# Hybrid convolution and sparse-attention block: intermediates stored in DRAM as high and low parts by their producers

## Chip, core and metric

One core of a Trainium2 chip runs the kernel as a single program. The metric is device time in microseconds (us), as the median of three executions. One further execution was recorded by the hardware profiler; all rows below come from it. Engine names are those of the profile: PE (TensorE), DVE (VectorE), ACT (ScalarE), POOL (GpSimd) and SP (the engine that issues almost all DMA transfers).

## What is computed

The input is x, 1024 tokens by 1024 channels, in float32. Cut to what matters here:

```python
h = rmsnorm(x, norm_in_g)
q, k, v..., gates, z_nsa, glu_in, z_conv, merge_g = split(h @ w_in)
o_nsa  = nsa_attention(q, k, v, gates, rel_bias)     # compressed + selected + window
y_nsa  = (o_nsa * silu(z_nsa)) @ w_nsa_proj
c      = silu(layernorm(dwconv31(a * sigmoid(b))))   # a, b = split(glu_in)
y_conv = (c * silu(z_conv)) @ w_conv_proj
g_conv, g_nsa = split(sigmoid(merge_g))
out    = rmsnorm(x + (g_conv * y_conv + g_nsa * y_nsa) @ w_out, norm_f_g)
```

There are 16 heads of width 64 in 2 key/value groups. All of it is held to float32 accuracy.

## The kernel before

**Three matmuls for one.** TensorE takes its operands here as `F32R` tiles, and one float32 product is built from three of them: weights high times activations high, high times low and low times high. The high part of a tile is an ACT `Copy` into an F32R tile; the low part is the float32 tile minus the high one, made by `sub_low` (line 68; the profile shows it as L69). Activations lie transposed, channels on partitions and tokens along the free axis, and are worked in two halves of 512 tokens (`hf`). A matrix of activations is four tiles, (high, low) by (half 0, half 1), each 128 x 8 x 512, taken from the tags b00, b01, b10 and b11 (`big_pair`).

**Stages.** Up to about 540 us of the span the kernel normalises x, projects it through `w_in` and runs the convolution. From there to about 1310 us the attention runs in eight steps (g, qp). TensorE's gaps between attention matmuls are filled with other projections, issued at a low priority: first the last columns of `w_in` (`late_columns`, L697), then `w_conv_proj` (`projections`, L964), then `w_nsa_proj` (`nsa_early`, L976). The bank for these fillers, `fb`, is one PSUM tile with one buffer. After 1310 us come the last part of `w_nsa_proj` and `w_out`.

**Order of the work.** Every engine runs its instructions in the order written by a scheduler at build time, from priorities in the code (`LOW`, `AHEAD`) and from `issue_after`, which ties the fillers of `nsa_early` to attention steps. SP issues its DMAs in one such order, too: a DMA that waits holds back all behind it.

**Intermediates in DRAM.** Four of them are written by one stage and read back by a later one as matmul operands:

- `YD`, the convolution path times its gate: made per half column in `late_columns` (L708 tanh on ACT, L710 on DVE, L712 the product with `ct` on POOL, L713 the store), read by `projections`.
- `OD`, the gated attention output: made per pair of heads in `attend` (L949 to L955, `ot`, one buffer), stored at L961, read for `nsa_early`.
- `ND`, the merged sum of both branches: made in `merged` (L677; L684 on DVE, L685 on POOL), stored at L982; half 0 is read back for `w_out` as `mh0` and `ml0`, half 1 as a partial sum (`mt`).
- `MD` and `GD` hold a partial sum and the gates, and are read as plain float32.

The tiles `mg`, `ct`, `gt`, `mt` and `sq` share the tag "ev", a ring of three buffers (L74): a new tile waits until the third one before it is done with. Reading YD, OD or ND half 0 goes through `load_half`: a DMA of a quarter (512 KB), an ACT copy to the high tile, and a subtraction on POOL (on DVE for `ml0`) that turns the loaded tile into the low part:

```python
nc.sync.dma_start(f(l), src[q * 256:(q + 1) * 256].rearrange("(k p) n -> p k n", p=P))
with tc.high_priority(offset=ahead):
    nc.scalar.activation(h, f(l), AF.Copy)
    sub_low(eng, l, f(l), h)
```

In `select` (L751 to L774 here) DVE scores the blocks of keys of the next attention step: row sums, a reciprocal, products over tiles of 128 x 312 and more, and the eight largest. DVE also makes the low parts `tl` of the transposed attention weights (L69), which TensorE needs for the attention output (L908).

Of the kernel before, what the change touches and what calls it, by code (L numbers as in the profile page):

```python
# [8 lines left out]
F32 = mybir.dt.float32  # L9
F32R = mybir.dt.float32r  # L10
AF = mybir.ActivationFunctionType
ALU = mybir.AluOpType
# [4 lines left out]
P = 128  # L17
S = 1024
D = 1024
KT = D // P  # L20
NB = S // P
HALF = 512
# [30 lines left out]
LOW = -1000000  # L53
AHEAD = 1000
# [4 lines left out]
def hybrid_block(ctx, tc, x, norm_in_g, w_in, pos_ck, w_ck1, w_ck2, pos_cv, w_cv1, w_cv2,  # L59
                 rel_bias, conv_w, conv_b, conv_ln_g, conv_ln_b, w_conv_proj, w_nsa_proj,  # L60
                 w_out, norm_f_g, cst, buckets, out):
    nc = tc.nc
    x, w_in, out = x[0], w_in[0], out[0]

    def f(ap):
        return ap.bitcast(F32)

    def sub_low(eng, low, full, high):
        eng.tensor_tensor(low, full, f(high), op=ALU.subtract)  # L69
# [4 lines left out]
    ev = ctx.enter_context(tc.tile_pool(name="ev", bufs=3, reuse_waits="tile"))  # L74
# [16 lines left out]
    OD = dram.tile([D, S], F32, name="OD")  # L91
    MD = dram.tile([D, S], F32, name="MD")
    CD = dram.tile([D, S], F32, name="CD")
    ND = dram.tile([2, D, HALF], F32, name="ND")
    TD = dram.tile([NH, P, 384], F32, name="TD")
    TV = dram.tile([NH, 384], F32, name="TV")

# [123 lines left out]
    with ExitStack() as c1:  # L221
# [302 lines left out]
        with ExitStack() as c2:  # L524
# [9 lines left out]
            for t in range(NB):  # L534
                ps = bank()
# [125 lines left out]
    def fbank():  # L661
        return pf.tile([P, HALF], F32, tag="f", name="fb")

    def load_half(pair, src, quarters, eng, ahead):
        ah, al = pair
        for q in quarters:
            ks = slice(2 * q, 2 * q + 2)
            h, l = ah[:, ks, :], al[:, ks, :]
            nc.sync.dma_start(f(l), src[q * 256:(q + 1) * 256].rearrange("(k p) n -> p k n", p=P))
            with tc.high_priority(offset=ahead):  # L670
                nc.scalar.activation(h, f(l), AF.Copy)
                sub_low(eng, l, f(l), h)

    def columns(w):
        return [w[0][:, t * P:(t + 1) * P] for t in range(KT)]

    def merged(t, hf, ps, prev, raise_, eng):  # L677
        sl = slice(hf * HALF, (hf + 1) * HALF)
        gt = ev.tile([P, HALF], F32, tag="ev", name="gt")
        nc.sync.dma_start(gt, GD[D + t * P:D + (t + 1) * P, sl])  # L680
        mt = ev.tile([P, HALF], F32, tag="ev", name="mt")
        nc.sync.dma_start(mt, prev)
        with tc.high_priority(offset=raise_):
            nc.vector.scalar_tensor_tensor(gt, gt, 1.0, ps, op0=ALU.add, op1=ALU.mult)  # L684
        eng.tensor_tensor(gt, gt, mt, op=ALU.add)  # L685
        return gt

    nsa_cols = columns(w_nsa_proj)
    oa = []
# [1 line left out]
    with att as c3:  # L691
# [5 lines left out]
        def late_columns():  # L697
            todo = [(C_ZC, t) for t in range(KT)] + [(C_MG, j) for j in range(EARLY, 2 * KT)]
            cols = [w_in[:, c + j * P:c + (j + 1) * P] for c, j in todo]
            for n, hf, ps in ends_halved(cols, hT, fbank, (False, True)):  # L700
                kind, j = todo[n]
                rows_j, sl = slice(j * P, (j + 1) * P), slice(hf * HALF, (hf + 1) * HALF)
                mg = ev.tile([P, HALF], F32, tag="ev", name="mg")
                if kind == C_ZC:
                    ct = ev.tile([P, HALF], F32, tag="ev", name="ct")
                    nc.sync.dma_start(ct, CD[rows_j, sl])
                with tc.high_priority(offset=-LOW):
                    nc.scalar.activation(mg, ps, AF.Tanh, scale=0.5)  # L708
                    if kind == C_ZC:
                        nc.vector.scalar_tensor_tensor(mg, mg, 1.0, ps, op0=ALU.add, op1=ALU.mult)  # L710
                if kind == C_ZC:
                    nc.gpsimd.tensor_tensor(mg, mg, ct, op=ALU.mult)  # L712
                    nc.sync.dma_start(YD[rows_j, sl], mg)  # L713
                else:
                    nc.sync.dma_start(GD[rows_j, sl], mg)

        with tc.high_priority(offset=LOW):
            late_columns()
# [195 lines left out]
        def attend(g, qp, sel, ahead):  # L914
            q, masks, pcs = sel
            nxt = None
            for hp in range(HG // 2):
# [26 lines left out]
                for u, (br, c, b) in enumerate(ones_):  # L944
# [4 lines left out]
                ot = ap.tile([P, 256], F32, tag="ot", name="ot", bufs=1)  # L949
# [6 lines left out]
                if (g, qp) == steps[-1]:  # L956
                    kk, to = g * 4 + hp, slice(qp % 2 * 256, (qp % 2 + 1) * 256)
                    nc.scalar.activation(oa[0][1][:, kk, to], ot, AF.Copy)
                    sub_low(nc.vector, oa[1][1][:, kk, to], ot, oa[0][1][:, kk, to])
                else:  # L960
                    nc.sync.dma_start(OD[fr, tk], ot)  # L961
            return nxt

        def projections():  # L964
            ya = big_pair()
            for hf in range(2):
                load_half((ya[0][hf], ya[1][hf]), YD[:, hf * HALF:(hf + 1) * HALF], range(4), nc.gpsimd, AHEAD)
            for t, hf, ps in ends_halved(columns(w_conv_proj), ya, fbank, (True, True)):
                sl = slice(hf * HALF, (hf + 1) * HALF)
                gt = ev.tile([P, HALF], F32, tag="ev", name="gt")  # L970
                nc.sync.dma_start(gt, GD[t * P:(t + 1) * P, sl])
                with tc.high_priority(offset=-2 * LOW):
                    nc.vector.scalar_tensor_tensor(gt, gt, 1.0, ps, op0=ALU.add, op1=ALU.mult)
                nc.sync.dma_start(MD[t * P:(t + 1) * P, sl], gt)

        def nsa_early():  # L976
            for hf in range(2):
                for t, src in enumerate(nsa_cols):
                    rows_t = slice(t * P, (t + 1) * P)
                    gt = merged(t, hf, mm_half(src, oa, hf, fbank(), (0, 1) if hf == 0 else (0,)),  # L980
                                MD[rows_t, hf * HALF:(hf + 1) * HALF], -2 * LOW, nc.gpsimd)
# [15 lines left out]
        for n, (g, qp) in enumerate(steps):  # L997
            if n in (2, 4, 6):
                load_bt(g)
            if n == 4:  # L1000
                base[0] = 0
                load_kv(0, 1, 1)
            if n == 6:
                load_kv(1, 0, 0)
                load_kv(1, 1, 1)
            if n == 6:
                with tc.high_priority(offset=2 * LOW):
                    projections()
                    oa.extend(big_pair())
                    load_half((oa[0][0], oa[1][0]), OD[:, 0:HALF], range(4), nc.gpsimd, AHEAD)  # L1010
                    load_half((oa[0][1], oa[1][1]), OD[:, HALF:S], range(2), nc.gpsimd, AHEAD)
                    while turns[0] < 0:
                        turns.pop(0)
                        next(early)
            if n == 7:
                with tc.high_priority(offset=2 * LOW):
                    load_half([m[:, :, 0:256] for m in (oa[0][1], oa[1][1])], OD[:, HALF:HALF + 256], range(2, 4),
                              nc.gpsimd, AHEAD)
# [9 lines left out]
    def ebank():  # L1028
        return pe.tile([P, HALF], F32, tag="e", name="eb")
# [1 line left out]
    gf = ep.tile([P, D], F32, name="gf", bufs=1)  # L1031
    mh = [big.tile([P, KT, HALF], F32R, tag="b00", name="mh0"), ep.tile([P, KT, HALF], F32R, name="mh1", bufs=1)]
    ml = [big.tile([P, KT, HALF], F32R, tag="b10", name="ml0"), ep.tile([P, KT, HALF], F32R, name="ml1", bufs=1)]
    load_half((mh[0], ml[0]), ND[0], range(4), nc.vector, 0)
    wo = [[ep.tile([P, KT, HALF], F32R, name=f"wo{part}{dh}", bufs=1) for part in range(2)] for dh in range(2)]

    def load_out(dh, q):
# [4 lines left out]
        sub_low(nc.vector, wo[dh][1][:, ks, :], raw, wo[dh][0][:, ks, :])  # L1042

    for t, src in enumerate(nsa_cols):
        gt = merged(t, 1, mm_half(src, oa, 1, ebank(), (1,)), ND[1, t * P:(t + 1) * P, :], 0, nc.vector)
        nc.scalar.activation(mh[1][:, t, :], gt, AF.Copy)
        sub_low(nc.vector, ml[1][:, t, :], gt, mh[1][:, t, :])
# [82 lines left out]
```

## Time and profile before

| | us |
|---|---|
| median of 3 executions | 1430.57 |
| lowest, highest | 1430.08, 1430.83 |
| the profiled execution's own time | 1430.01 |
| span from its first to its last instruction | 1428.2 |
| mean granted TensorE clock | 0.994 of full speed |

A row of the profile gives start and length in microseconds and names the engine, the line of the code, and output and inputs of the instruction. "Waits" are the stretches in which an engine stood still, with the instruction that ended the wait. In windows each engine has its busy time, with the number of instructions in brackets; PEclk is the granted TensorE clock, and the last two columns are the mean busy share of the DMA engines and what they moved in GB/s.

### The profile page before, as it was taken

To read this page: it belongs to the slowest core of one execution; us is meant where nothing else is said; L and a number is where in the kernel's file an instruction comes from. 1 tells how busy PE (TensorE), PEld (TensorE's weight loads), DVE (VectorE), ACT (ScalarE), POOL (GpSimd) and SP (SyncE) were. 2 spreads that over 40 slices of the span, in tenths; PEclk is the share of its full clock that TensorE was granted. 3 is DMA by queue.
4 is the path that set the end of the run, shared out by engine and by line. 5 is a ranking of instruction groups with operands and counts; after the bars stand their busy time and mean duration, and the time that the engine had idled before them with its cause. 6 is when DMAs were issued, how large, how long until landed. Compare 5 with 4: busy or idle time off the path is not lost.

```text
span 1428.2 us, 22832 instructions
## 1 busy us (share of the span) xinstructions
PE 1391.0 (97%) x7516; PEld 1197.0 (84%) x7516; DVE 1032.8 (72%) x2367; ACT 675.4 (47%) x1441; POOL 709.6 (50%) x809
## 2 busy tenths in 40 slices
PE   6999999999999999999999999989999999999997
PEld 5788888888988787889888889879989898898786
DVE  5699999999965714767676685586678557886732
ACT  6321112113144424766656666755555766675421
POOL 2323224234155825765555455785545887884111
PEclk9999999999999999999999999999999999999999
DMA  5333424346283743343333322453253543534632
GB/s 174 72 104 106 128 69 133 113 132 176 81 199 111 236 122 113 119 128 101 96 94 89 115 83 59 130 170 115 89 148 119 178 129 123 182 115 153 219 119 89
DMA packets 189167, 179.55 MB, mean 126 GB/s; under 512 B 12549, under 2 KB 146773, under 8 KB 189048
## 3 DMA queue, kind: packets, MB, share of 16 engines
q1 hardware_dynamic: 186984, 174.94, 40.7%
q10 hardware_dynamic: 2064, 3.15, 0.7%
q8 instruction: 60, 0.98, 0.3%
q14 instruction: 59, 0.48, 0.1%
HBM read 128.20 MB, written 52.98 MB: 127 GB/s over the span
## 4 chain that ended last, share of the span: by engine, by line
PE 82%; DVE 6%; DMA 4%; issue 3%; POOL 3%; ACT 2%; SPq 0%; ACTq 0%; DVEq 0%; POOLq 0%
PE mm L122 9%; PE mm L124 9%; PE mm L123 9%; PE sb L835 7%; PE tb L882 7%; PE fb L122 4%; PE fb L123 4%; PE fb L124 4%; PE ob L908 3%; PE ob L907 3%; PE fb L134 3%; PE fb L135 3%; PE fb L136 3%; PE eb L1063 2%; PE eb L1062 2%
## 5 line engine op out<-in xcount | busy, mean ns | idle before, releaser
L69 POOL TENSOR_TENSOR wl<-raw,wh 128x512 fp32r<-128x512 f32 x184 | 244.9, 1332 | 371.4 <-ACT wh L111 360.1
L353 DVE SCALAR_TENSOR_TENSOR ca<-u,vec,ca 128x1024 f32<-128x1024 f32 x232 | 284.0, 1281 | 0.8
L122 PE MATMUL mm<-act,wh 128*128 128x512 f32 x640 | 252.9, 395 | 1.5 <-DVE zs L566 1.3
L123 PE MATMUL mm<-act,wh 128*128 128x512 f32 x640 | 249.6, 390 | 0.0
L124 PE MATMUL mm<-act,wl 128*128 128x512 f32 x640 | 247.2, 390 | 0.0
L870 ACT ACTIVATE p<-p,ac 128x640 f32<-128x640 f32 (+7 forms) x256 | 187.5, 735 | 88.0 <-DVE ac L862 82.4
L111 ACT ACTIVATE wh<-raw 128x512 fp32r<-128x512 f32 x184 | 115.4, 628 | 232.0 <-PE mm L123 157.9
L875 POOL TENSOR_SCALAR p<-p,rcx,gates 128x640 f32<-128x640 f32 (+7 forms) x256 | 201.4, 797 | 8.9
L69 DVE TENSOR_TENSOR tl<-tb,th 128x512 fp32r<-128x512 f32 (+1 forms) x272 | 158.0, 591 | 46.1 <-ACT th L886 44.5
L835 PE MATMUL sb<-k,q 128*128 128x384 f32 (+2 forms) x704 | 176.5, 350 | 2.5 <-DVE ac L862 1.5
L886 ACT ACTIVATE th<-tb 128x512 fp32r<-128x512 f32 (+1 forms) x272 | 135.0, 517 | 70.8 <-PE tb L882 66.6
L882 PE MATMUL tb<-ident,p 128*128 128x128 f32 x1056 | 165.1, 273 | 0.1
L122 PEld LDWEIGHTS mm<-act,wh 128*128 128x128 f32 x640 | 120.1, 188 | 27.6 <-DVE zs L566 1.8
L124 PEld LDWEIGHTS mm<-act,wl 128*128 128x128 f32 x640 | 120.1, 188 | 25.9 <-POOL wl L69 0.6
L123 PEld LDWEIGHTS mm<-act,wh 128*128 128x128 f32 x640 | 120.2, 188 | 24.7
L122 PE MATMUL fb<-act,wh 128*128 128x512 f32 x320 | 127.9, 400 | 2.5 <-ACT mg L708 1.3
L882 PEld LDWEIGHTS tb<-ident,p 128*128 128x128 f32 x1056 | 124.7, 140 | 4.7 <-DVE stl L69 0.3
L908 PE MATMUL ob<-tl,v 128*128 128x256 f32 x448 | 124.0, 297 | 4.1 <-DVE tl L69 3.8
L124 PE MATMUL fb<-act,wl 128*128 128x512 f32 x320 | 126.2, 394 | 0.0
L123 PE MATMUL fb<-act,wh 128*128 128x512 f32 x320 | 126.1, 394 | 0.0
L907 PE MATMUL ob<-th,v 128*128 128x256 f32 x448 | 124.2, 291 | 1.0 <-ACT th L886 0.9
L835 PEld LDWEIGHTS sb<-k,q 128*128 128x128 f32 x704 | 114.1, 189 | 12.8 <-DVE ac L862 2.8
(245 smaller groups left out, 2638.9 us busy)
## 6 DMA issues: line engine op xcount, KB each, us to landing
raw<-in_w_in_dram SPq DMA_DIRECT2D x128, 256.0 KB, 3.1
gt<-GD SPq DMA_DIRECT2D x40, 256.0 KB, 3.1
GD<-mg SPq DMA_DIRECT2D x32, 256.0 KB, 3.3
q<-QD SPq DMA_DIRECT2D x64, 128.0 KB, 3.6
raw<-in_w_nsa_proj_dram SPq DMA_DIRECT2D x32, 256.0 KB, 3.0
raw<-in_w_conv_proj_dram SPq DMA_DIRECT2D x24, 256.0 KB, 3.7
k<-KD SPq DMA_DIRECT2D x40, 128.0 KB, 3.5
xt<-in_x_dram SPq DMA_DIRECT2D x8, 512.0 KB, 6.2
```

Of the source, the lines that this page charges most:

```text
L69: eng.tensor_tensor(low, full, f(high), op=ALU.subtract)
L122: nc.tensor.matmul(ps, wh[:, k, :], mh[:, kk, :], start=(kk == 0), stop=False)
L123: nc.tensor.matmul(ps, wh[:, k, :], ml[:, kk, :], start=False, stop=False)
L124: nc.tensor.matmul(ps, wl[:, k, :], mh[:, kk, :], start=False, stop=(kk == KT - 1))
L353: nc.vector.scalar_tensor_tensor(dst, u, w, accs[e], op0=ALU.mult, op1=ALU.add)
L835: nc.tensor.matmul(s[:, 0:w], lhs, K[j][:, br, k0:k0 + w], start=(j == 0), stop=(j == 1))
L870: nc.scalar.activation(pt[:, 0:n], pt[:, 0:n], AF.Exp, bias=mn, scale=-1.0, accum_out=sm[:, b:b + 1])
L875: nc.gpsimd.tensor_scalar(pt[:, 0:n], pt[:, 0:n], rc[:, b:b + 1], gates[:, 2 * qp + b, gcol:gcol + 1], op0=ALU.mult, op1=ALU.mult)
L882: nc.tensor.transpose(tp[:, j * P:(j + 1) * P], src, ident)
L886: nc.scalar.activation(th, src, AF.Copy)
L907: nc.tensor.matmul(dst, lhs, th[:, sl], start=False, stop=False)
L908: last = nc.tensor.matmul(dst, lhs, tl[:, sl], start=False, stop=False)
```

## The change

YD and OD become arrays of two parts, high and low. ND keeps only half 1, and half 0 moves to a new array `NS` of two parts. The stage that makes a value also splits it (`split_store`) and stores both parts; the reader loads two tiles (`load_pair`) and does no arithmetic. The tiles on the ring "ev", `ot`, and a new tile `oh` (one buffer) become F32R. Where a high part needs a tile, a used one serves: `ct` for YD and `mt` for NS.

```diff
-    YD = dram.tile([D, S], F32, name="YD")
+    YD = dram.tile([2, D, S], F32, name="YD")
...
-    def load_half(pair, src, quarters, eng, ahead):
...
+    def load_pair(pair, src, quarters):
         for q in quarters:
+            for part in range(2):
+                nc.sync.dma_start(f(pair[part][:, 2 * q:2 * q + 2, :]),
+                                  src[part, q * 256:(q + 1) * 256].rearrange("(k p) n -> p k n", p=P))
+
+    def split_store(high, low, dst):
+        nc.scalar.activation(high, f(low), AF.Copy)
+        sub_low(nc.gpsimd, low, f(low), high)
+        nc.sync.dma_start(dst[0], f(high))
+        nc.sync.dma_start(dst[1], f(low))
...
-                    nc.gpsimd.tensor_tensor(mg, mg, ct, op=ALU.mult)
-                    nc.sync.dma_start(YD[rows_j, sl], mg)
+                    nc.gpsimd.tensor_tensor(f(mg), f(mg), f(ct), op=ALU.mult)
+                    split_store(ct, mg, YD[:, rows_j, sl])
...
-                    nc.sync.dma_start(OD[fr, tk], ot)
+                    oh = ap.tile([P, 256], F32R, tag="oh", name="oh", bufs=1)
+                    split_store(oh, ot_, OD[:, fr, tk])
...
-                    nc.sync.dma_start(ND[hf, rows_t, :], gt)
+                    if hf == 0:
+                        split_store(mt, gt, NS[:, rows_t])
+                    else:
+                        nc.sync.dma_start(ND[rows_t], f(gt))
...
-    load_half((mh[0], ml[0]), ND[0], range(4), nc.vector, 0)
+    load_pair((mh[0], ml[0]), NS, range(4))
```

**How instructions move.** Three places are shown, before and then after; the lines of the changed kernel are shifted by 3 or 4. First POOL, at the step in which the loads of YD used to be split; `wl<-raw,wh` makes a weight's low part, `p<-p,rcx,gates` scales attention weights, `act<-act` is the subtraction of `load_half`:

```order
L69 TENSOR_TENSOR wl<-raw,wh 128x512
L69 TENSOR_TENSOR act<-act 128x1024
L875 TENSOR_SCALAR p<-p,rcx,gates 128x640
L875 TENSOR_SCALAR p<-p,rcx,gates 128x768
L69 TENSOR_TENSOR act<-act 128x1024
L69 TENSOR_TENSOR wl<-raw,wh 128x512
L69 TENSOR_TENSOR act<-act 128x1024 x2
L771 TENSOR_TENSOR lt<-lt,gates 128x8x39
```

```order
L959 TENSOR_TENSOR ot<-ot,zt 128x256
L69 TENSOR_TENSOR wl<-raw,wh 128x512
L851 TENSOR_TENSOR cm<-bt,msk 128x256
L69 TENSOR_TENSOR ot<-ot,oh 128x256
L69 TENSOR_TENSOR wl<-raw,wh 128x512
L851 TENSOR_TENSOR cm<-bt,msk 128x256
L875 TENSOR_SCALAR rcx<-rcx 128x2
L878 TENSOR_SCALAR p<-p,rcx,gates 128x640
```

The subtractions on 128 x 1024 are gone, and a subtraction on 128 x 256 stands behind each product of `ot`. Second DVE at the same step, where `select` scores the blocks (L766, L767 and L770 before are L769, L770 and L773 after):

```order
L766 TENSOR_TENSOR lt<-lt,rc 128x8x39
L862 ISA p,ac<-sb,bt,ac 128x256
L862 ISA ac 128x1
L767 SCALAR_TENSOR_TENSOR lt<-lt 128x8x39
L751 TENSOR_REDUCE sm<-lt 128x8
L770 TENSOR_REDUCE ih<-lt 128x39
L69 TENSOR_TENSOR tl<-tb,th 128x512
L752 TENSOR_SCALAR sm<-sm 128x8
```

```order
L769 TENSOR_TENSOR lt<-lt,rc 128x8x39
L769 TENSOR_TENSOR lt<-lt,rc 128x8x47
L865 ISA p,ac<-sb,cm,ac 128x256
L865 ISA ac 128x1
L770 SCALAR_TENSOR_TENSOR lt<-lt 128x8x39
L770 SCALAR_TENSOR_TENSOR lt<-lt 128x8x47
L773 TENSOR_REDUCE ih<-lt 128x39
L773 TENSOR_REDUCE ih<-lt 128x47
```

The scoring of two blocks of queries, which was spread over some 30 rows, now stands together. Third SP, at the loads of `mh0` and `ml0`:

```order
L669 DMA ml_15074<-ND 128x2x512 x3
L103 DMA raw<-in_w_nsa_proj_dram 128x4x128
L982 DMA ND<-gt 128x512
L682 DMA mt<-MD 128x512
L680 DMA gt<-GD 128x512
L669 DMA ml_15074<-ND 128x2x512
```

```order
L668 DMA ml_15243<-NS 128x2x512
L668 DMA mh_15241<-NS 128x2x512 x2
L668 DMA ml_15243<-NS 128x2x512
L668 DMA mh_15241<-NS 128x2x512
L104 DMA raw<-in_w_nsa_proj_dram 128x4x128
L668 DMA ml_15243<-NS 128x2x512
L674 DMA NS<-mt 128x512
L675 DMA NS<-gt 128x512
L104 DMA raw<-in_w_nsa_proj_dram 128x4x128
L685 DMA mt<-MD 128x512
L668 DMA mh_15241<-NS 128x2x512
L683 DMA gt<-GD 128x512
L668 DMA ml_15243<-NS 128x2x512
```

Three loads ahead of the last store of half 0 have become six, and that store has become two.

In all, ACT loses 16 copies of quarters of YD and OD and 4 of ND and gains 24 copies on 128 x 512 and 28 on 128 x 256; POOL loses 16 subtractions of quarters and gains 24 on 128 x 512 and 28 on 128 x 256; DVE loses 4; SP issues 72 more DMAs (16 + 28 + 8 stores and 8 + 8 + 4 loads). TensorE's instructions are the same in number.

## Rows read from the trace of the kernel before

**Rows 1.** The page's first part: busy time of each engine over the span.

```profile
PE 1391.0 (97%) x7516; PEld 1197.0 (84%) x7516; DVE 1032.8 (72%) x2367; ACT 675.4 (47%) x1441; POOL 709.6 (50%) x809
```

**Rows 2.** What TensorE waited for, 545 to 1310 us: us, times, longest.

```profile
PE ob L908 <- DVE tl L69: 3.8, 4, 2.9
PE sb L835 <- DVE ac L862: 1.5, 3, 0.8
...
PE fb L122 <- ACT mg L708: 1.3, 2, 0.9
...
PE fb L122 <- DVE mg L710: 0.9, 2, 0.6
```

**Rows 3.** Windows: length, PE, PEld, DVE, ACT, POOL busy, PEclk, DMA share, GB/s.

```profile
940.00:945.40 5.40, 1.68 (x10) 1.00 (x8) 5.37 (x9) 3.66 (x7) 5.40 (x4) 0.86 0.54 185
945.40:950.90 5.50, 5.28 (x17) 4.24 (x18) 5.50 (x14) 1.52 (x3) 5.50 (x4) 0.52 0.29 91
...
1120.00:1140.00 20.00, 19.32 (x116) 16.64 (x116) 11.70 (x38) 13.67 (x30) 19.00 (x19) 1.00 0.53 170
```

**Rows 4.** Timeline of DVE, 939 to 953 us: start, length, engine, line.

```profile
939.47 0.39 DVE L752 TENSOR_SCALAR sm<-sm 128x8 f32<-128x8 f32 x1
...
941.46 2.24 DVE L767 SCALAR_TENSOR_TENSOR lt<-lt 128x312 f32<-128x312 f32 x1
...
945.26 1.91 DVE L752 TENSOR_SCALAR sm<-sm 128x8 f32<-128x8 f32 x1
...
952.27 0.54 DVE L767 SCALAR_TENSOR_TENSOR lt<-lt 128x376 f32<-128x376 f32 x1
```

**Rows 5.** Timeline of POOL, 936 to 950 us.

```profile
940.77 2.58 POOL L69 TENSOR_TENSOR act<-act 128x1024 fp32r<-128x1024 f32 x1
...
944.79 4.68 POOL L69 TENSOR_TENSOR act<-act 128x1024 fp32r<-128x1024 f32 x2
```

**Rows 6.** Groups by line, 545 to 1310 us: busy us, mean ns, idle before and releaser.

```profile
L69 POOL TENSOR_TENSOR act<-act 128x1024 fp32r<-128x1024 f32 (+1 forms) x16 | 36.1, 2269 | 4.5 <-ACT act L671 4.4
L671 ACT ACTIVATE act<-act 128x1024 fp32r<-128x1024 f32 (+1 forms) x16 | 16.1, 1004 | 9.7 <-DMA act<-YD 4.9 <-DMA act<-OD 4.8
L69 DVE TENSOR_TENSOR ml<-ml,mh 128x1024 fp32r<-128x1024 f32 x4 | 5.3, 1336 | 0.9 <-ACT mh L671 0.9
L69 POOL TENSOR_TENSOR wl<-raw,wh 128x512 fp32r<-128x512 f32 x88 | 115.2, 1309 | 61.6 <-ACT wh L111 56.4 <-DMA ct<-CD 3.4
L955 POOL TENSOR_TENSOR ot<-ot,zt 128x256 f32<-128x256 f32 x31 | 22.9, 740 | 31.1 <-DVE ot L954 30.7
```

**Rows 7.** The page's costliest groups: the ACT copy on 128 x 512.

```profile
L111 ACT ACTIVATE wh<-raw 128x512 fp32r<-128x512 f32 x184 | 115.4, 628 | 232.0 <-PE mm L123 157.9
```

**Rows 8.** The chain that ended last, near 1120 us: start, us, what.

```profile
1119.83 2.39 POOL act L69
```

**Rows 9.** Timeline of SP's queue, 555 to 585 us.

```profile
557.32 0.33 SPq L713 DMA_DIRECT2D YD<-mg  x1
561.09 0.33 SPq L706 DMA_DIRECT2D ct<-CD  x1
...
565.91 0.45 SPq L713 DMA_DIRECT2D YD<-mg  x1
```

**Rows 10.** Instructions on the tile mg, 540 to 710 us: ns min/median/max, first and last start.

```profile
L708 ACT ACTIVATE mg<-fb x16: 575/584/600, 544.8 to 701.8; 128x512 f32<-128x512 f32 x16
```

**Rows 11.** Timeline of SP's queue, 1228 to 1250 us.

```profile
1229.30 1.39 SPq L669 DMA_DIRECT2D ml<-ND  x3
...
1232.62 0.33 SPq L982 DMA_DIRECT2D ND<-gt  x1
...
1238.29 0.32 SPq L680 DMA_DIRECT2D gt<-GD  x1
```

**Rows 12.** Timeline of DVE, 1238 to 1246 us.

```profile
1243.46 1.28 DVE L69 TENSOR_TENSOR ml<-ml,mh 128x1024 fp32r<-128x1024 f32 x1 [0.91 <-ACT mh L671]
1244.67 0.68 DVE L684 SCALAR_TENSOR_TENSOR gt<-gt,fb 128x512 f32<-128x512 f32 x1
```

**Rows 13.** Window while three of those loads run, columns as in rows 3.

```profile
1231.00:1233.00 2.00, 2.00 (x17) 1.91 (x16) 1.30 (x4) 1.89 (x5) 1.81 (x4) 1.00 1.02 390
```

More of the change, by code (lines that the diff above doesn't have):

```diff
@@ L88, in hybrid_block @@
     ZD = dram.tile([D, S], F32, name="ZD")
-    YD = dram.tile([D, S], F32, name="YD")
+    YD = dram.tile([2, D, S], F32, name="YD")
     GD = dram.tile([2 * D, S], F32, name="GD")
-    OD = dram.tile([D, S], F32, name="OD")
+    OD = dram.tile([2, D, S], F32, name="OD")
     MD = dram.tile([D, S], F32, name="MD")
     CD = dram.tile([D, S], F32, name="CD")
-    ND = dram.tile([2, D, HALF], F32, name="ND")
+    ND = dram.tile([D, HALF], F32, name="ND")
+    NS = dram.tile([2, D, HALF], F32, name="NS")
     TD = dram.tile([NH, P, 384], F32, name="TD")
@@ L662, in fbank @@
         return pf.tile([P, HALF], F32, tag="f", name="fb")
-    def load_half(pair, src, quarters, eng, ahead):
-        ah, al = pair
+    def load_pair(pair, src, quarters):
         for q in quarters:
[L667 to L672, printed above, removed]
+            for part in range(2):
[6 more added lines that the diff above has]
+        nc.sync.dma_start(dst[1], f(low))
     def columns(w):
@@ L678, in merged @@
         sl = slice(hf * HALF, (hf + 1) * HALF)
[L679 to L682, printed above, removed]
+        gt = ev.tile([P, HALF], F32R, tag="ev", name="gt")
+        nc.sync.dma_start(f(gt), GD[D + t * P:D + (t + 1) * P, sl])
+        mt = ev.tile([P, HALF], F32R, tag="ev", name="mt")
+        nc.sync.dma_start(f(mt), prev)
         with tc.high_priority(offset=raise_):
-            nc.vector.scalar_tensor_tensor(gt, gt, 1.0, ps, op0=ALU.add, op1=ALU.mult)
-        eng.tensor_tensor(gt, gt, mt, op=ALU.add)
-        return gt
+            nc.vector.scalar_tensor_tensor(f(gt), f(gt), 1.0, ps, op0=ALU.add, op1=ALU.mult)
+        eng.tensor_tensor(f(gt), f(gt), f(mt), op=ALU.add)
+        return gt, mt
     nsa_cols = columns(w_nsa_proj)
@@ L948, in attend @@
                     nc.tensor.matmul(dst, lhs, stl[:, u], start=False, stop=u == len(ones_) - 1)
-                ot = ap.tile([P, 256], F32, tag="ot", name="ot", bufs=1)
+                ot_ = ap.tile([P, 256], F32R, tag="ot", name="ot", bufs=1)
+                ot = f(ot_)
                 lo, hi = slice(0, DK), slice(DK, P)
@@ L966, in projections @@
             for hf in range(2):
-                load_half((ya[0][hf], ya[1][hf]), YD[:, hf * HALF:(hf + 1) * HALF], range(4), nc.gpsimd, AHEAD)
+                load_pair((ya[0][hf], ya[1][hf]), YD[:, :, hf * HALF:(hf + 1) * HALF], range(4))
             for t, hf, ps in ends_halved(columns(w_conv_proj), ya, fbank, (True, True)):
@@ L979, in nsa_early @@
                     rows_t = slice(t * P, (t + 1) * P)
-                    gt = merged(t, hf, mm_half(src, oa, hf, fbank(), (0, 1) if hf == 0 else (0,)),
-                                MD[rows_t, hf * HALF:(hf + 1) * HALF], -2 * LOW, nc.gpsimd)
-                    nc.sync.dma_start(ND[hf, rows_t, :], gt)
+                    gt, mt = merged(t, hf, mm_half(src, oa, hf, fbank(), (0, 1) if hf == 0 else (0,)),
+                                    MD[rows_t, hf * HALF:(hf + 1) * HALF], -2 * LOW, nc.gpsimd)
+                    if hf == 0:
+                        split_store(mt, gt, NS[:, rows_t])
+                    else:
+                        nc.sync.dma_start(ND[rows_t], f(gt))
                     yield
@@ L1009, in hybrid_block @@
                     oa.extend(big_pair())
-                    load_half((oa[0][0], oa[1][0]), OD[:, 0:HALF], range(4), nc.gpsimd, AHEAD)
-                    load_half((oa[0][1], oa[1][1]), OD[:, HALF:S], range(2), nc.gpsimd, AHEAD)
+                    load_pair((oa[0][0], oa[1][0]), OD[:, :, 0:HALF], range(4))
+                    load_pair((oa[0][1], oa[1][1]), OD[:, :, HALF:S], range(2))
                     while turns[0] < 0:
@@ L1016, in hybrid_block @@
                 with tc.high_priority(offset=2 * LOW):
-                    load_half([m[:, :, 0:256] for m in (oa[0][1], oa[1][1])], OD[:, HALF:HALF + 256], range(2, 4),
-                              nc.gpsimd, AHEAD)
+                    load_pair([m[:, :, 0:256] for m in (oa[0][1], oa[1][1])], OD[:, :, HALF:HALF + 256], range(2, 4))
             part = select(*steps[n + 1]) if n + 1 < len(steps) else None
```

18 lines of the change are left out of this document (9 added, 9 removed).

## Prediction, made before the changed kernel was run

> **What bounds the kernel now.** I read the busy times first: TensorE is busy for 1391.0 of 1428.2 us, VectorE for 72% and GpSimd for 50% [rows 1]. A change that leaves TensorE's instructions alone can win only what TensorE loses while it waits, or while its clock is low, and can cost only by making it wait more. So the next view is what TensorE waited for once the attention had begun. The list is short [rows 2]: the longest entry is the low part `tl` from VectorE, 3.8 us, of which one wait is 2.9; waits for the accumulators `ac` make 1.5, with one of 0.8; and the late columns make 2.2 (tanh and gate product, `mg`). The windows show where the two large ones lie [rows 3]. From 940.0 to 945.4 us TensorE is busy for 1.68 of 5.40 us, and in the 5.5 us after that its granted clock is 0.52, nearly the lower level of 1.2 GHz instead of 2.4. Before the stall it had run at the upper level. That is 3.7 us idle, 0.2 idle behind, and 5.28 us of work at half speed, of which 2.5 are lost (5.28 x 0.48): **6.4 us in all**.
>
> The timeline of VectorE says why [rows 4]. It is full there, and two small instructions of `select` are far too long: L767 takes 2.24 us, against 0.54 ten us later on a larger tile, and L752 takes 1.91, against 0.39 just before. L767 ends at 943.70 and L752 at 947.17. On GpSimd [rows 5] a subtraction of `load_half` on 128 x 1024 ends at 943.35, and the first of the next two (4.68 us for both) at about 947.13. VectorE's instruction ends with GpSimd's, twice, so I read them as held by it. The holds make 1.70 + 1.52 = 3.2 us of the 3.9 idle, that is 82%.
>
> **The change part by part.**
>
> *The splits at the loads go.* GpSimd loses 36.1 us in 16 subtractions of 2.27 us, ScalarE 16 copies of 1.00, VectorE 5.3 us [rows 6]. None of this is on TensorE's path except where it holds somebody up. Around 940 us no such subtraction is left (the order of GpSimd shows none), so I take 82% of the stall away: 6.4 x 0.82 = **-5.2**. Bounds: all of it, -6.4; and -1.4, if the weight subtractions that stay do the holding (second rival).
>
> *OD's splits* stand on the chain that ended last, 2.39 us near 1120 us [rows 8], where GpSimd is busy for 19.0 of 20 us and TensorE idles 0.68 [rows 3]. The split of OD's loads is what crowds GpSimd: **-0.7**, between -0.7 and 0.
>
> *The split of ml0 on VectorE* held L684, which empties TensorE's only `fb` bank: a wait of 0.91 and 1.28 of work stand just before it [rows 12]. Most was hidden by the queue: **-0.5**, between -0.9 and 0.
>
> *New splits at the producers.* GpSimd gets 24 subtractions on 128 x 512 at 1.31 us, priced by the same operation on weights, and 28 on 128 x 256 at 0.74, priced by L955 [rows 6]: 31.4 + 20.7 = 52.1 us, or 16 more than it loses. ScalarE gets at most 52 copies at 0.63 [rows 7], 33 us. VectorE loses work. GpSimd is busy for half of the span, and TensorE's list of waits [rows 2] names it nowhere, so this lies beside other work; if that cover went, 28 scaled attention weights could each come 0.74 us late. I take **+0.3**, between 0 and +2.
>
> The Trainium skill, "SBUF — State Buffer", section "SBUF: two separate sides", says that VectorE and GpSimd share a port pair as an exclusive lock: whichever starts first keeps it for its whole instruction and the other blocks. That agrees with rows 4 and 5, and speaks against this change as well, as 52 new subtractions can take the lock where 16 did; by it the holds get shorter, 1.31 or 0.74 in place of 2.27, but more frequent.
>
> *Late columns.* `ct` now holds its slot of the ring until the high part has landed, and `mg` until the low part has. Loads of the next `ct` wait for that slot. From one YD store to the next that round takes 565.91 - 557.32 = 8.6 us [rows 9]. The change adds the subtraction, 1.31, and one issue, 0.33: 10.2 us. Half columns come every (701.8 - 544.8) / 15 = 10.5 us [rows 10], so it just fits on average, not in each round: **+1**. Bounds: 0, as TensorE never waited for the store before; and +8.8, if each round loses another 0.8 us in SP's queue (third rival). Queued behind a waiting store on SP are loads of q and of weights, which are issued well before use.
>
> *Loads of NS.* Before the last store of half 0 stood three loads, now six [rows 11], and the store waits for a copy and a subtraction. At the 390 GB/s of that time [rows 13] a load of 512 KB takes 1.34 us, so three more are 4.0, and the split 0.63 + 1.31 = 1.9: 5.9 us later. Behind it wait the next `mt` and `gt`, on which TensorE's `fb` bank hangs. That `gt` was issued at 1238.29 and used at 1244.67 [rows 11, 12], after some 3 us of transfer, so 3 to 4 us of the 5.9 are slack. I take **+1.5**; bounds 0 and +8.4 (first rival).
>
> The 72 further DMAs cost SP about 0.33 us each [rows 9], 24 us on an engine that does nothing else: nothing beyond the above.
>
> **Sum:** -5.2 - 0.7 - 0.5 + 0.3 + 1 + 1.5 = -3.6. Against the profiled execution's 1430.01 that is 1426.4. The median of the runs shown is 0.56 higher, so I predict **1427.0 us**.
>
> **The rivals.**
>
> *1. The NS loads make TensorE wait (slower).* No slack for `gt`: TensorE waits for the 5.9 us, and then loses 2.5 to the lower clock, as after the stall at 940. That is 8.4 in place of 1.5, so 1433.9. For it: SP's queue is in order, and the six loads stand ahead of the stores. Against: TensorE's order puts more attention work there. It decides once `gt` lands over 4 us later than before.
>
> *2. The hold passes to others (no change).* GpSimd still has weight subtractions of 1.31 us near 940 us, and VectorE's order puts the scoring of two blocks together, so it is denser. Then only the difference in length is won, 3.2 x (2.27 - 1.31) / 2.27 = 1.4, and the low clock stays: -1.4 in place of -5.2, so 1430.8. For it: VectorE is busy for 5.37 of 5.40 us there [rows 3] and remains so. By the lock of the page named above this is the case to expect wherever a weight subtraction meets the scoring.
>
> *3. The late columns fall behind (slower).* Each of 16 rounds takes 11.0 us instead of 10.2, against 10.5 available: 16 x 0.55 = 8.8 in place of 1, so 1434.8. For it: the slack is 0.3 us. Against: TensorE's waits on `mg` were small, and the bank is freed before the store.
>
> *4. More is won.* The stall goes whole (-6.4) with the other two gains, none of the three costs shows, and VectorE's other waits in rows 2 go too (3.8 - 2.9 + 1.5 - 0.8 = 1.6): -9.2, so 1421.4.
>
> That the change does not do what it says I give nothing: the order shows loads without arithmetic.
>
> **How the numbers follow.** A measurement of this kernel can tell some 0.2% from no change, 2.9 us: faster means below 1427.7, slower above 1433.4. Forecast 0.42, with a range of its own from 1423.5 to 1431: it splits into 0.30 faster, 0.11 same, 0.01 slower. Rival 1 0.12, slower. Rival 2 0.19: 0.02 faster, 0.15 same, 0.02 slower. Rival 3 0.12, slower. Rival 4 0.15, faster. Together 0.47 faster, 0.26 same, 0.27 slower. The range goes from 1421.0, which leaves out about half of rival 4, to 1435.5, which takes in the centres of rivals 1 and 3 and leaves out the rest of them.
>
> **What would show it.** Right: no wait of TensorE over 1 us between 920 and 960 us and a granted clock of 1.00 there; L770 of the changed kernel (L767 before) at about 0.5 us everywhere; no wait for `gt` near 1240 us. Rival 1: a wait of TensorE's L134-type fillers on `gt` near 1235 to 1250 us with the clock at 0.5 behind it. Rival 2: `tl` late again, somewhere from 900 to 960 us, with `select` long on VectorE beside a weight subtraction on GpSimd. Rival 3: waits of `fb` on `mg` between 545 and 705 us well over 2.2 us. The forecast is wrong as a whole if the time is outside its own range, or inside it with the stall at 940 us still there.

## The result and the profile after

The changed kernel takes **1439.14 us** (median of six executions, 1436.27 to 1443.03) against 1430.70 before in the same comparison. The ratio is 1.0059, with a 95% interval from 1.0047 to 1.0071: **8.4 us slower**. Forecast were 1427.0 us and a gain; the time lies above the range, too, which ended at 1435.5. Below, a difference in microseconds is the ratio less one, times 1430.6, and so need not equal the difference of two medians.

The page's first part has, for the profiled execution of the changed kernel (1436.83 us, near the lower end of the six; span 1435.0):

```profile
PE 1394.0 (97%) x7516; PEld 1197.6 (83%) x7516; DVE 1032.3 (72%) x2363; ACT 680.5 (47%) x1473; POOL 723.4 (50%) x845
```

Against [rows 1] GpSimd has 14 us more (16 were forecast), and TensorE the same work. So the time is in the waits. The view of TensorE's waits from 545 to 1310 us (total, times, longest) answers to [rows 2]:

```profile
PE ob L911 <- DVE tl L69: 3.2, 7, 0.7
PE tb L885 <- POOL p L878: 3.0, 2, 2.3
PE sb L838 <- DVE ac L865: 2.1, 4, 0.9
PE tb L885 <- DVE stl L69: 1.6, 2, 0.9
```

The one long wait for `tl` (2.9) is gone and seven short ones stand there. A new entry names GpSimd: `p L878`, the scaled attention weights, 2.3 us at once. The windows of 20 us show where (length, then busy time of PE, PEld, DVE, ACT and POOL, PEclk, DMA share and GB/s):

```profile
600.00:620.00 20.00, 18.62 (x100) 15.26 (x99) 17.03 (x71) 15.01 (x39) 13.81 (x19) 1.00 0.46 141
680.00:700.00 20.00, 17.69 (x98) 14.29 (x97) 13.38 (x46) 11.68 (x34) 10.17 (x17) 1.00 0.37 114
940.00:960.00 20.00, 18.75 (x116) 16.07 (x115) 19.11 (x57) 11.61 (x23) 7.28 (x8) 1.00 0.77 263
960.00:980.00 20.00, 18.79 (x113) 16.47 (x112) 16.34 (x58) 12.22 (x25) 14.73 (x21) 1.00 0.40 126
1080.00:1100.00 20.00, 18.05 (x109) 15.27 (x109) 19.85 (x55) 9.58 (x20) 12.36 (x14) 1.00 0.42 129
1120.00:1140.00 20.00, 20.00 (x127) 18.09 (x126) 14.58 (x46) 13.28 (x29) 12.59 (x17) 1.00 0.74 244
1240.00:1260.00 20.00, 16.42 (x101) 14.09 (x100) 13.18 (x37) 10.06 (x22) 12.86 (x15) 0.91 0.77 240
```

The same windows of the kernel before are these (the one at 1120 us is in [rows 3]):

```profile
600.00:620.00 20.00, 19.96 (x107) 16.55 (x106) 16.11 (x68) 15.70 (x41) 12.87 (x19) 1.00 0.37 108
680.00:700.00 20.00, 19.23 (x114) 16.29 (x113) 11.03 (x45) 11.11 (x35) 10.06 (x16) 1.00 0.27 81
940.00:960.00 20.00, 16.05 (x81) 13.38 (x80) 19.76 (x52) 10.62 (x20) 16.94 (x16) 0.83 0.34 109
960.00:980.00 20.00, 20.00 (x124) 17.89 (x124) 13.74 (x48) 13.16 (x28) 14.38 (x19) 1.00 0.48 146
1080.00:1100.00 20.00, 20.00 (x123) 17.91 (x122) 16.84 (x50) 11.51 (x25) 13.09 (x16) 1.00 0.38 119
...
1240.00:1260.00 20.00, 19.19 (x119) 16.65 (x118) 16.58 (x52) 13.31 (x27) 16.78 (x19) 1.00 0.61 196
```

Counting as lost what TensorE was idle, and of its busy time the share by which its clock fell short, the stretch from 940 to 980 us loses 6.7 us before and 2.5 after: 4.2 won. The stretch from 1120 us wins the 0.7. Lost are 1.3 at 600, 1.5 at 680, 2.0 at 1080 and **4.3 at 1240 us**. That makes +4.2 of the 6.8 us between the two profiled executions. Over the whole span the same count has 46.7 us lost against 41.7 before, that is +5.0, of which 1.9 lie after 1300 us; the other 1.8 us it does not place.

The largest piece can be read in full. SP's queue of the changed kernel around 1230 us:

```profile
1231.20 0.89 SPq L668 DMA_DIRECT2D ml<-NS  x1
1232.19 1.16 SPq L674 DMA_DIRECT2D NS<-mt  x1
1233.45 0.54 SPq L675 DMA_DIRECT2D NS<-gt  x1
...
1240.84 0.32 SPq L685 DMA_DIRECT2D mt<-MD  x1
...
1241.72 0.42 SPq L683 DMA_DIRECT2D gt<-GD  x1
```

and GpSimd's timeline behind it, with TensorE's next instruction:

```profile
1244.16 1.26 POOL L688 TENSOR_TENSOR gt<-gt,mt 128x512 f32<-128x512 f32 x1 [4.02 <-DMA mt<-MD]
1245.41 2.27 POOL L878 TENSOR_SCALAR p<-p,rcx,gates 128x896 f32<-128x896 f32 x2
```

```profile
1246.56 0.33 PE L885 MATMUL tb<-ident,p 128*128 128x128 f32 x1 [2.35 <-POOL p L878]
```

The high part sits in `mt`, so `mt`'s slot of the ring stays taken until its store has landed. That store was issued at 1232.19 behind six loads of NS; the next `mt<-MD` went out at 1240.84, 8.6 us later. The waits of SP's queue from 545 to 1310 us say that it waited for that store; the longest of the three, 5.2 us, is this one:

```profile
SPq L685 <- DMA NS<-mt: 9.1, 3, 5.2
```

In the kernel before the load went out 0.4 us after the store of `gt` [rows 11]:

```profile
1232.99 0.43 SPq L682 DMA_DIRECT2D mt<-MD  x1
```

GpSimd stood for 4.02 us at the sum of `gt` and `mt`, and the attention weights queued behind it kept TensorE for 2.35 us, after which its clock fell (0.50 from 1248 to 1250 us, 0.91 over the whole window).

### The profile page after: what moved, and what is told of

It is laid out like the page before. It is cut to its first block, busy times and chain, and to the rows that moved or that the text cites. A ratio compares the mean times of both kernels' runs of the same rounds, so it can differ in the third digit from the quotient of the medians.

```text
span 1435.0 us, 22971 instructions
## 1 busy us (share of the span) xinstructions
PE 1394.0 (97%) x7516; PEld 1197.6 (83%) x7516; DVE 1032.3 (72%) x2363; ACT 680.5 (47%) x1473; POOL 723.4 (50%) x845
## 5 line engine op out<-in xcount | busy, mean ns | idle before, releaser
L878 POOL TENSOR_SCALAR p<-p,rcx,gates 128x640 f32<-128x640 f32 (+7 forms) x256 | 200.5, 794 | 8.5
```

The costliest lines, as they stand in the source:

```text
L878: nc.gpsimd.tensor_scalar(pt[:, 0:n], pt[:, 0:n], rc[:, b:b + 1], gates[:, 2 * qp + b, gcol:gcol + 1], op0=ALU.mult, op1=ALU.mult)
```

## The experiments

**One part of the change at a time** (five runs). Each kernel takes one or two of YD, OD and NS as two parts and leaves the others as before: the lines of the diff ahead that touch them are undone, and `load_half` is kept for their loads.

NS alone:

> Only ND half 0 is stored as two parts (NS); YD and OD as in the kernel before. Theory 1 (the wait of the changed kernel near 1240 us is made by NS: the tile mt keeps its slot of the ring until its store, queued behind the loads of NS, has landed, and GpSimd stands still for the next mt with attention weights queued behind it): the stall at 940 us stays as before, and near 1240 us there is a wait of GpSimd for mt of about 4 us and of TensorE of 2 to 3 us with a lower clock behind it; 4 to 7 us slower than before, 1435 to 1438. Rival (the order of all engines shifts with any edit and the collisions of GpSimd and VectorE move about): near 1240 us no wait over 1 us, and a time anywhere between 1428 and 1434.

Measured: 1431.01 us, ratio 1.0002 (0.9993 to 1.0011), no difference. GpSimd's wait is there, and longer than in the changed kernel:

```profile
POOL gt L698 <- DMA mt<-MD: 4.8, 1, 4.8
```

But TensorE is busy for 19.04 of the 20 us from 1240 on (19.19 before). So theory 1 was right about the wait and wrong about its price: behind the sum stood a product of `ot` and a weight's low part, and no attention weights that TensorE needed soon.

YD alone:

> Only YD is stored as two parts. Theory 1 (the subtractions on 128 x 1024 at the loads of YD hold VectorE at 940 us): the stall there goes, about 4.6 us, and the new subtractions of mg cost 1 to 3 us between 545 and 705 us; so 1427 to 1429. Rival (order shifts, collisions move): the stall at 940 goes, but others of the same kind appear elsewhere, in places where no instruction of the change stands; 1429 to 1434.

Measured: 1431.78 us, ratio 1.0001 (0.9991 to 1.0010). The stall at 940 shrank as in the changed kernel, and the gain was lost again between 580 and 620 us (1.6), from 960 (1.4) and at 1254 us, where TensorE waited 2.34 us for `th` behind ScalarE's copy of a load of ND. That is the rival's picture.

OD alone:

> Only OD is stored as two parts. Theory 1: the stall at 940 us stays (6.4 us), the 0.7 to 1.5 us near 1120 us go, and the 28 new subtractions of ot cost 2 to 4 us in the attention, most of it at 603 and 683 us; so 1432 to 1434. Rival (the producers of YD, not of OD, make the new waits at 603 and 683 us): those two waits are not there and the time is 1429 to 1430.

Measured: 1437.59 us, ratio 1.0042 (1.0029 to 1.0054), 6.0 us slower, so **OD is the dear part** in this order. The waits at 603 and 683 us are not there, against theory 1. The stall at 940 stayed, and a new one stands where ScalarE waits for a load of ND that is split by its reader as before (the array is called NS in this run):

```profile
1234.16 1.06 ACT L672 ACTIVATE mh<-ml 128x1024 fp32r<-128x1024 f32 x1 [4.11 <-DMA ml<-NS]
```

```profile
1241.13 0.58 PE L920 MATMUL ob<-th,v 128*128 128x256 f32 x1 [2.75 <-ACT th L899]
```

From 1220 to 1260 us 7.4 us are lost, against 0.8 before, so in this trace the loss is not at the new subtractions.

YD and OD, and YD and NS:

> YD and OD as two parts, ND half 0 as before: the change without its NS part. Theory 1: the wait near 1240 us goes, and with it 4 to 7 of the 8.4 us; 1432 to 1435. Rival (the loss lies in the producers' splits of YD and OD, and the stall at 1240 is only where a lost slack shows): 1437 to 1440, with the loss moved elsewhere.

> YD and NS as two parts, OD as before: the change without its OD part. Theory 1 (OD's part is the costly one: 7.0 us in the run with OD alone; YD alone and NS alone cost nothing): 1429 to 1432, no difference to before. In the run with YD alone TensorE waited 2.3 us at 1254 us behind a copy of ND's loads on ScalarE, which this kernel does not have, so that wait is gone here. Rival (each part costs what the schedule makes of it, parts do not add): 1434 to 1438.

Measured: 1435.30 us (1.0036, 1.0023 to 1.0048) with OD, and 1430.56 us (0.9998, 0.9988 to 1.0007) without it. Without OD the change is neutral; with OD it costs 5 to 6 us; and NS on top of both costs another 3.3 (1.0059 against 1.0036), although it is free alone. What a new order costs by itself is measured further down, and 3.3 is not above it.

**The loads of NS moved.** Each quarter is issued behind a store of ND, some 30 to 50 us later:

```diff
-                        nc.sync.dma_start(ND[rows_t], f(gt))
+                        st_ = nc.sync.dma_start(ND[rows_t], f(gt))
...
+                        if t in (2, 3, 4, 5):
+                            with tc.issue_after(st_.ins):
+                                load_pair(m0, NS, [(2, 3, 4, 5).index(t)])
...
-    load_pair((mh[0], ml[0]), NS, range(4))
```

> The changed kernel whole, with one thing moved: the eight loads of NS are issued one quarter at a time behind the stores of ND for t = 2 to 5 (near 1260 to 1295 us) instead of in one burst before the last store of NS. Theory 1 (the burst of 3 MB delays the store that frees the tile mt; GpSimd stands still for the next mt, and attention weights behind it): the wait of GpSimd near 1240 us and TensorE's 2.35 us behind it go, the clock stays at its upper level there, and 4 to 6 us are won: 1433 to 1435, as for the change without its NS part (1435.3). Rival (the wait is only where slack runs out; the loss comes back further on): 1437 to 1440, with the wait moved to 1260 to 1310 us.

Measured: 1433.23 us, ratio 1.0017 (1.0008 to 1.0026), **6.0 us less** than the changed kernel. The list of GpSimd's waits from 1225 to 1265 us has no `mt` any more, and the window reads:

```profile
1240.00:1260.00 20.00, 19.24 (x130) 17.47 (x129) 15.77 (x52) 13.74 (x29) 15.50 (x19) 1.00 0.57 174
```

So the burst of loads made this wait, and the loss did not come back elsewhere (41.8 us lost over the span, against 46.7). What the wait costs depends on what else is queued: with OD's subtractions on VectorE (next but one) the same move wins 3.3 us in one order and 0.6 in another.

**The hold of VectorE by GpSimd.** In the kernel before, each subtraction of `load_half` was cut in two:

```diff
-                sub_low(eng, l, f(l), h)
+                for k in range(2):
+                    sub_low(eng, l[:, k], f(l[:, k]), h[:, k])
```

> The kernel before, with one thing changed: each subtraction of load_half (on GpSimd, and on VectorE for ml0) is made as two instructions on 128 x 512 instead of one on 128 x 1024. Same work. Theory 1 (an instruction of VectorE that meets a GpSimd subtraction ends only with it, so the hold is as long as what is left of that one instruction): no VectorE instruction of select near 940 us is over 1.5 us (2.24 and 1.91 before), and of the 6.4 us lost at 940 to 951 us 1 to 4 are won: 1427 to 1429.5. Rival (the two ends coincide by chance, and VectorE waits for something else): the two instructions stay at about 2 us and the time at 1430.

Measured: 1437.72 us, ratio 1.0037 (1.0025 to 1.0050), slower by 5.3 us. The two instructions of `select` did get shorter; their groups (ns min/median/max; the lines are shifted by one) have at most 1037 and 1252 ns, against 1905 and 2236 before [rows 4]:

```profile
L753 DVE TENSOR_SCALAR sm<-sm x16: 153/168/1037, 517.6 to 1085.2; 128x8 f32<-128x8 f32 x16
```

```profile
L768 DVE SCALAR_TENSOR_TENSOR lt<-lt x8: 470/612/1252, 741.6 to 1090.8; 128x312 f32<-128x312 f32 x2, 128x376 f32<-128x376 f32 x2, 128x440 f32<-128x440 f32 x2, 128x504 f32<-128x504 f32 x2
```

The hold is as long as what is left of GpSimd's instruction; that much of theory 1 stands. But the stall is not smaller:

```profile
940.00:960.00 20.00, 13.75 (x70) 10.45 (x70) 19.90 (x53) 10.52 (x19) 19.28 (x20) 0.97 0.43 130
```

TensorE has 13.75 busy microseconds there at a clock of 0.97, before 16.05 at 0.83; counted as above, 6.7 us are lost in both, and 3.0 more from 960 us, where none were. The profiled execution is the slowest of this kernel (1441.37). VectorE is at 19.90 us, 19.76 before, and many short holds stand there: five instructions on 128 x 16 tiles from 950 to 955 us take 0.7 to 1.3 us, where one of that size took 0.16 in the kernel before. How much of the 5.3 us is the new order alone is not shown.

**OD's subtractions on VectorE.**

```diff
-                    split_store(oh, ot_, OD[:, fr, tk])
+                    split_store(oh, ot_, OD[:, fr, tk], nc.vector)
```

`split_store` takes the engine of its subtraction as a fourth argument here.

> The changed kernel, with the 28 subtractions of ot on VectorE (0.41 us each) instead of GpSimd (0.74). Theory 1 (the new subtractions on GpSimd hold VectorE and make the waits at 603, 683 and 1085 to 1098 us, some 6 us): these waits shrink and 3 to 6 us are won, 1433 to 1436, with the wait at 1240 us still there. Rival (VectorE is full in the attention, so 11.5 us more work on it costs as much): 1438 to 1442.

> Only OD as two parts (as in the run that came out at 1437.6), with the 28 subtractions of ot on VectorE instead of GpSimd. Theory 1 (OD's price is the GpSimd time of its producers): 3 to 7 us less than 1437.6, that is 1430 to 1434, with the stall at 940 us still there, since YD's loads are split as before. Rival (the price lies at 1235 us, where ScalarE waits for a load of ND with attention weights behind it, and has nothing to do with the engine of the subtraction): 1436 to 1439 with the wait of 2.75 us on th near 1240 us.

Measured: 1427.89 us for the whole change (0.9984, 0.9975 to 0.9993), **10.7 us less** than with the 28 subtractions on GpSimd, and 1430.98 us for OD alone (0.9998, 0.9989 to 1.0007), 6.3 less. In the whole change the gain is larger than theory 1 gave it, although an instruction takes longer there than the 0.41 I had assumed:

```profile
L69 DVE TENSOR_TENSOR ot<-ot,oh 128x256 fp32r<-128x256 f32 x28 | 18.0, 642 | 3.5 <-ACT oh L672 3.4
```

**Is it only the order?** Every edit makes the scheduler write another order. 32 tiny GpSimd instructions without use were added to measure what that alone does:

```diff
+                scr = ap.tile([P, 2], F32, tag="scr", name="scr", bufs=2)
+                nc.gpsimd.tensor_scalar(scr, ot[:, 0:2], 1.0, None, op0=ALU.mult)
```

> The kernel before with 32 tiny GpSimd instructions added (128 x 2, one behind each product of ot, about 0.2 us each, result unused). Hardly any work, but the scheduler writes another order for every engine. Theory 1 (the 8.4 us come from the work that the change adds): 1429 to 1432, no difference to before. Rival (any new order moves the collisions of GpSimd, VectorE and DMA, and costs or wins several us by itself): more than 3 us away from before, either way.

> The changed kernel with the same 32 tiny GpSimd instructions. Theory 1: 1438 to 1441, with the wait near 1240 us in its place. Rival: more than 3 us away from the changed kernel's 1439, with the waits at 603, 683 and 1085 us gone or elsewhere.

> The changed kernel with the subtractions of ot on VectorE (1427.9) in a second order: the 32 tiny GpSimd instructions of the null runs added. If the engine makes the difference: 1426 to 1431, at least 6 us under the changed kernel in its second order (1437.2). If the order does: 1432 to 1438.

> OD alone as two parts with the subtractions on GpSimd (1437.6) in a second order, with the same 32 tiny instructions. If GpSimd makes the difference to VectorE (1431.0): 1435 to 1440. If the order does: 1430 to 1434.

| kernel | us | ratio to before | in the second order: us | ratio |
|---|---|---|---|---|
| before | 1430.6 | 1 | 1434.06 | 1.0026 (1.0017 to 1.0035) |
| changed | 1439.14 | 1.0059 | 1437.16 | 1.0046 (1.0034 to 1.0058) |
| OD alone, on GpSimd | 1437.59 | 1.0042 | 1436.03 | 1.0035 (1.0022 to 1.0048) |
| changed, OD's subtractions on VectorE | 1427.89 | 0.9984 | 1429.80 | 0.9994 (0.9985 to 1.0002) |

An order costs up to 4 us by itself: the rival is right so far, and no difference under that can be put down to a single edit here. Within the second order the changed kernel is 2.9 us slower than the kernel before, and OD alone 1.3, so what of the 8.4 and 6.0 us is the change's own is not known more closely. The engine's difference is larger. It is 10.7 us in one order and 7.4 in the other, and 8.0 with the loads of NS moved (1.0017 against 0.9961, the best version below).

The traces say where it lies. Counted as above, TensorE loses in the windows at 600, 680, 960 (which is also in the 4.2 us won above), 1080 and 1100 us together:

| kernel | us lost |
|---|---|
| before | 0.8 |
| YD's and OD's subtractions on GpSimd: changed, without NS, with the loads of NS moved, in the second order | 6.9, 6.8, 6.7, 10.8 |
| OD's on VectorE: changed, with the loads of NS moved, and each in the second order | 1.6, 1.7, 1.9, 2.2 |

OD alone does not show this: there the same windows lose 1.3 us with the subtractions on GpSimd (5.6 in the second order) and 4.0 on VectorE.

TensorE's waits for `tl`, `stl` and `p` from 545 to 1310 us are 5.1 to 7.8 us in the versions of the second row and 1.3 to 1.8 in those of the third. In the changed kernel `tl` has 3.2 us and `p` 3.0; with OD's subtractions on VectorE these are left:

```profile
PE ob L911 <- DVE tl L69: 0.7, 2, 0.4
PE tb L885 <- POOL p L878: 0.6, 1, 0.6
```

Then the same work without use, 28 subtractions of full size in the kernel before, on GpSimd or (`nc.vector`) on VectorE:

```diff
+                if (g, qp) != steps[-1]:
+                    scr = ap.tile([P, 256], F32, tag="scr", name="scr", bufs=1)
+                    nc.gpsimd.tensor_tensor(scr, ot, zt, op=ALU.subtract)
```

> The kernel before with 28 subtractions on 128 x 256 added on GpSimd (0.74 us each, 20.7 in all), one behind each product of ot, result unused; nothing is stored or loaded in addition. Theory 1 (GpSimd's time behind the product of ot costs TensorE): 1434 to 1439, as with OD's part alone (1437.6). Rival (only a new order costs, whatever the work): as far from before as the tiny instructions were, 1431 to 1435, or anywhere, but the same as with the work on VectorE.

> The same 28 unused subtractions on VectorE (0.41 us each, 11.5 in all) in the kernel before. Theory 1: VectorE is asked for less time and lets GpSimd go on, 1429 to 1433, and at least 3 us less than with the same work on GpSimd. Rival: the same as on GpSimd within 2 us, as both change the order.

Measured: 1433.66 us (1.0027, 1.0015 to 1.0038) on GpSimd and 1434.59 us (1.0038, 1.0024 to 1.0052) on VectorE. Theory 1 fell here: work for which nobody waits costs 3.9 and 5.4 us, the same on both engines within the intervals, and about as much as the tiny instructions (3.7). So in this kernel, which has no subtractions of `mg`, it is not GpSimd's time as such. The engine mattered where the subtraction stands between the product of `ot` and the two stores. SP's queue is not the way, by the rows: it waited longer for that subtraction on VectorE (9.1 and 5.1 us in the two orders) than on GpSimd (5.3 and 4.4). Whether the holds of VectorE, GpSimd's queue or the tile `ot` with its one buffer make `tl`, `stl` and `p` late was not separated.

**The best version** has both edits that won, the loads of NS moved and OD's subtractions on VectorE. It was run as it is, in the second order, and with the subtractions of `mg` moved to VectorE in the same way:

> The changed kernel with both edits that won singly: subtractions of ot on VectorE (1427.9 alone) and the loads of NS behind the stores of ND (1433.2 alone, against 1439.1). Theory 1: with the first edit TensorE still waited 2.35 us near 1256 us for gt with a loss of 2.6 us in that stretch; the second takes 1.5 to 3 us of it: 1425 to 1427. Rival (the new order makes other waits): 1428 to 1433.

> The fastest kernel so far (1425.5: subtractions of ot on VectorE, NS loaded late) with the 32 tiny GpSimd instructions of the null runs. Theory 1 (the gain comes from the work and where it is queued): 1424 to 1429, faster than before by more than 1.5 us still. Rival (the 1425.5 is a lucky order): 1429 or more.

> The fastest kernel so far with the 16 subtractions of mg on VectorE as well (0.69 us each) instead of GpSimd (1.31). Theory 1 (GpSimd's new work is what costs): 0 to 3 us less, 1422.5 to 1425.5; before it, TensorE lost 7.5 us between 540 and 620 us in that kernel. Rival (VectorE is the engine that TensorE waits for in that stretch, so more work on it costs): 1426 to 1430.

Measured: **1425.48 us** (0.9961, 0.9948 to 0.9974), 5.6 us less than before; in the second order 1427.72 us (0.9990, 0.9982 to 0.9999), 1.4 us less with an interval that ends just below 1; the rest hangs on the order. With the subtractions of `mg` on VectorE as well it is 1433.97 us (1.0034, 1.0021 to 1.0047), on the rival's side and beyond its figures. That VectorE is what the late columns wait for is not shown by it: from 540 to 620 us that kernel loses 5.8 us, the best version 4.6 (not the 7.5 of the expectation), and most of the difference lies elsewhere. In the best version the window from 1240 us is full and the clock is up:

```profile
1240.00:1260.00 20.00, 20.00 (x126) 18.07 (x125) 15.17 (x48) 13.65 (x29) 17.96 (x22) 1.00 0.49 158
```

## Why the prediction was wrong

- **The stall at 940 us.** Right: -5.2 forecast, 4.2 won in the window; the 0.7 near 1120 us came as said. It is not a matter of the order: from 940 to 980 us all nine traces in which YD is split by its reader lose 6.3 to 9.7 us, and all eleven in which its producer splits it 1.7 to 4.7. The group of the scoring instruction shows the shorter hold:

```profile
L770 DVE SCALAR_TENSOR_TENSOR lt<-lt x8: 467/641/957, 745.7 to 1092.9; 128x312 f32<-128x312 f32 x2, 128x376 f32<-128x376 f32 x2, 128x440 f32<-128x440 f32 x2, 128x504 f32<-128x504 f32 x2
```

  At most 957 ns, against 2236, where I had said about 0.5 us everywhere. The low parts `tl` are still late there by 0.7 us, so the second rival holds in part. Of the two instructions that I read as held, the first ended 0.35 us after GpSimd's (943.70 and 943.35) and only the second with it.
- **The split of `ml0`: -0.5.** It does not show: TensorE's waits for `gt` from that line are 0.6 us (L687), and were 0.3 (L684).
- **New splits at the producers: +0.3, at most +2. This step failed.** With YD's and OD's subtractions on GpSimd TensorE loses some 6 us more than before in the five windows of the table above (10 in the second order), and 7 to 11 us are won by moving OD's 28 to VectorE. Neither +0.3 nor +2 was worked out: the 28 late weights that I named would be 20.7 us. I took GpSimd's new work as covered because GpSimd is busy for half of the span (it is 64% from 545 to 1310 us) and because TensorE's list of waits named it nowhere. The list names who came last, and GpSimd acts on TensorE through others: it holds VectorE, and its queue is in order. I had named the more frequent holds, and put no price on them. At 600 us this is plain. On GpSimd of the changed kernel the new subtractions of `mg` and `ot` stand back to back:

```profile
599.75 1.33 POOL L69 TENSOR_TENSOR mg<-mg,ct 128x512 fp32r<-128x512 f32 x1
601.03 0.74 POOL L69 TENSOR_TENSOR ot<-ot,oh 128x256 fp32r<-128x256 f32 x1
```

```profile
600.08 1.02 DVE L763 SCALAR_TENSOR_TENSOR rg<-rc,cs,gates 128x8 f32<-128x8 f32 x1
...
601.21 0.63 DVE L767 TENSOR_TENSOR lt<-lt,rg 128x56 f32<-128x56 f32 x1
```

  Two instructions of VectorE on small tiles end with them, at 601.10 and 601.84, and `stl` and `tl` come late behind them: the 1.3 us of that window. In the kernel before the same two (L760 and L764 there) had no GpSimd instruction beside them:

```profile
598.71 0.23 DVE L760 SCALAR_TENSOR_TENSOR rg<-rc,cs,gates 128x8 f32<-128x8 f32 x1
...
599.13 0.21 DVE L764 TENSOR_TENSOR lt<-lt,rg 128x56 f32<-128x56 f32 x1
```

  The losses at 680 and 1080 us stand mostly beside weight subtractions that were there before. Yet they recur in all four versions with both splits on GpSimd (2.1 to 2.5 and 0.9 to 2.0 us), and in the four with OD's on VectorE they are 1.1 to 1.3 and at most 0.05. So they go with OD's split on GpSimd, where YD is split by its producer too; through which instructions is not shown.
- **NS: +1.5, at most +8.4. Too small here.** The burst and the fallen clock of the first rival, where it said, and too small a chance (0.12). The size was 4.3 us in the window and 6.0 by the run with the loads moved; but in the second order of the changed kernel GpSimd stands as long at that sum (4.0 us), and the windows at 1240 and 1260 us lose only 1.7. I named `gt` as the late tile; it was `mt`, and TensorE's 2.35 us were a wait for attention weights, with 0.59 for `gt` behind it. For the late columns I had worked out that the high part keeps its tile until the store lands, and did not apply this to `mt`. Nor did I ask what stands on GpSimd behind the sum of `gt` and `mt`.
- **Late columns: +1.** The third rival did not happen: the waits for `mg` are 1.2 and 0.9 us, as in [rows 2].
- **The order.** The sum treats the rest of the program as fixed. The runs with useless instructions moved their kernels by between 1.9 us down and 5.4 us up. With a forecast of -3.6 the chance of a loss should have been larger for that alone.

The Trainium skill, "SBUF — State Buffer", section "Who interferes with whom", says that of a VectorE instruction with two inputs in SBUF, or in a two-port mode, and a GpSimd instruction that reads SBUF the one that starts first blocks the other for its whole length. The rows of VectorE at 600 us (1.02 us against 0.23) and the shortened holds of the run with halved subtractions (at most 1.25 us against 2.24) agree with it. From the rule alone I had expected less time with the shorter holds; the run shows 5.3 us more.

## What to carry to other kernels

Moving a split from the reader to the producer moves a wait as well: a tile that holds a part to be stored is free only when the store has landed, and with a burst of loads issued just before, that took over 8 us here. Whether such a wait costs anything is decided by what is queued behind it on that engine; a wait of 4 to 5 us was free in one kernel, and 4.3 us were lost with it in another. An engine that no wait of TensorE names is not free for that: ask whom it holds up. And before a gain of a few microseconds is put down to an edit of a scheduled kernel, the same edit is best run in a second order: useless instructions alone cost 4 to 5 us in the kernel before.

## What the runs showed of the hardware that was not expected

An instruction of VectorE on a 128 x 8 tile (L752, in the changed kernel L755) took 0.17 us by its median, but up to 1.9 us before and up to 1.29 after, beside a GpSimd subtraction. A subtraction of `ot` on 128 x 256 took 0.64 us on VectorE in the mean and 0.74 on GpSimd: in the attention VectorE is hardly the faster engine, yet with these 28 on it the kernel runs 6 to 11 us faster. After waits of 2.35 and 0.59 us TensorE's granted clock fell to 0.50, the lower level, as it had to 0.52 after the 2.9 us of the kernel before [rows 3].
